# A hybrid decoder block with PEER: other engines for the first conditioning parts and for the gate table

## The chip, the cores and the metric

The kernel runs on one core of a Trainium2 chip. The metric is the device time of one execution, from the first to the last instruction of the core. Three runs of the kernel before took 2813.15, 2819.97 and 2822.08 us, so the median is 2819.97 us.

## The reference

One decoder layer for 1024 tokens of width 1024 in float32. A condition vector c gives six vectors of shifts, scales and gates. The mixing part runs one projection whose columns are shared by a gated convolution and by window attention; the channel part retrieves, for each token, 8 heads x 16 single-neuron experts out of 128 x 128. Cut to what matters:

```python
cond = silu(c);  mod = cond @ w_ada + b_ada;  sh1, sc1, g1, sh2, sc2, g2 = split(mod, 6)
h  = rms_norm(x, norm1_g) * (1 + sc1) + sh1
b_gate, c_gate, hc, q, k, v = split(h @ w_in)
y_conv = b_gate * conv3_causal(c_gate * hc)
y_attn = window_attention(rms_norm(q), rms_norm(k), v, rel_bias, sinks)   # window 128, bias by T5 buckets
x  = x + g1 * (concat(group_norm(y_conv), group_norm(y_attn)) @ w_out)
h2 = rms_norm(x, norm2_g) * (1 + sc2) + sh2
# PEER: 8 heads, product keys 128 x 128, top 16 of 16384 experts per head
q  = h2 @ wq;  scores with keys[0], keys[1];  top 16 of each;  top 16 of the 256 sums -> eidx, softmax -> g
a  = gelu(u[eidx] . h2)
x  = x + g2 * sum_k (g * a)_k v[eidx_k]
```

## The kernel before

The tokens go through the mixing part in three groups (`front`): 384, 384 and 256. Float32 accuracy comes from splitting an operand into a high part rounded to fp32r and a low part, and summing three fp32r products (H.H, L.H, H.L): that is line 301 for the projections, 864 and 921 for the experts. The retrieval ends in one of two ways. For tokens 0 to 639 all 16384 experts are multiplied (`dense`, from about 1010 us on), with a table of gates that is zero where an expert isn't chosen. For tokens 640 to 1023 the chosen rows of u and v are gathered by GpSimd's indirect DMAs beside the dense part.

**The gate table.** For each of five blocks of 128 tokens, `select` (line 625 on) finds the chosen experts as two indices and a gate, and `spread` (line 715) writes the table. Per token the table is a 128 x 128 matrix, and it is an outer product over the 128 chosen slots: `oi` (slot x first index, one-hot times the gate) as weights and `oj` (slot x second index, one-hot) as moving operand. `make(k)` builds these for four tokens, `multiply(k)` does four matmuls into one PSUM tile `gps` (two buffers), `evict(k)` copies it on ScalarE into `stage`, and after eight k the stage goes out to DRAM (`gd`). A block is thus 32 steps k in four stages, and one stage buffer means that the first eviction of the next stage waits until the DMA of the last one is done. The pattern `HOT = "APVV"` gives the four `oi` of each step to ScalarE (two instructions, lines 735 and 736), GpSimd (one) and VectorE (two tokens, one instruction each, line 738); VectorE also makes `oj` for all four in one instruction (line 742). The `oi` have 8 buffers, two steps' worth.

**The start.** `ada_start` (line 184) computes the first two parts of the modulation. Part 1 (scale) is summed on VectorE from eight 128 x 1024 tiles of w_ada (line 193) and then reduced over partitions on TensorE by a matmul with ones (line 200). Part 0 (shift) goes through TensorE alone: 64 fp32 matmuls with one column each (line 195). Meanwhile GpSimd multiplies x by its inverse norm (line 1086). Then `norm1` writes hH and hL, and the projections of the first group begin. The table of attention biases (`bias_table`, line 207) is made beside these projections: eight fp32 matmuls of 384 columns (line 218), each followed by a VectorE addition of the mask and a DMA.

**What sets the order.** Each engine runs its own instructions strictly in the order in which they stand. A scheduler of the framework sets that order when the program is built, except inside `tc.manual_schedule`, where the order is that of the code (in the kernel before that holds for the steady part of `dense`). The steps of `select` and `spread` are a background task: `bg` advances it by `SPREAD = 0.94` steps per estimated us of projection work of the next group, so that the table of group 1's blocks is written beside the projections of group 2 and so on. The order thus fixed does not adapt: where a matmul of `multiply` waits for its `oi`, the projections behind it wait too.

## Time and profile before

| | |
|---|---|
| runs (us) | 2822.08, 2819.97, 2813.15 |
| profiled execution (us) | 2812.93 |
| its span (us) | 2811.2 |
| mean granted TensorE clock | 0.979 |
| PE busy | 2684.1 us, 95% |
| DVE busy | 2287.5 us, 81% |
| ACT busy | 1090.8 us, 39% |
| POOL busy | 1439.0 us, 51% |

PE is TensorE, PEld its weight loads, DVE is VectorE, ACT is ScalarE, POOL is GpSimd. The shares are means over stages with different limits: the dense part is 1.8 of the 2.8 ms. A line of the groups gives engine, operation, out<-in, shapes, the count, then busy us and mean ns of one, then the idle time of the engine just before these instructions and what ended most of it. An fp32 matmul shows as two weight loads and two matmuls.

### The profile page before, as it was taken

Reading aid. Unit: us, or ns where it says so; the run is one execution under the profiler, and the core shown is the slowest. Engines: PE = TensorE matmul, PEld = TensorE weight load, DVE = VectorE, ACT = ScalarE, POOL = GpSimd, SP = SyncE. Lnnn points to the kernel's source line nnn. Section 1 sums busy time; section 2 is a strip of 40 time slices with the busy share of each in tenths; the row PEclk is TensorE's granted clock in tenths of the full one; section 3 lists DMA queues with packets and bytes.
Section 4 is the critical chain, followed back from the end, with each engine's and each line's share of the span. In section 5 each row is a group of like instructions: output and inputs, shape, how many; then the busy total and the mean of one; then the engine's idle time right before and its main releaser. Section 6 shows DMA issues by size and latency. Waiting matters only on the chain.

```text
span 2811.2 us, 45327 instructions
## 1 busy us (share of the span) xinstructions
PE 2684.1 (95%) x15679; PEld 2443.0 (87%) x15679; DVE 2287.5 (81%) x4845; ACT 1090.8 (39%) x2201; POOL 1439.0 (51%) x1323
## 2 busy tenths in 40 slices
PE   8898999999888889999999999999999999999998
PEld 6777989889788788999989899989988899889997
DVE  3664899777987687888988888888888888898886
ACT  2454479774788433232223222322222222222321
POOL 3443433320333145666666566666665666566661
PEclk7999999999999989999999999999999999999999
DMA  7878755677667868999999999999999999999995
GB/s 243 270 245 283 249 198 197 219 256 247 218 212 276 293 224 288 355 329 330 336 341 337 330 360 332 331 332 346 338 314 326 344 340 338 327 337 335 331 332 178
DMA packets 381445, 830.39 MB, mean 295 GB/s; under 512 B 35328, under 2 KB 134048, under 8 KB 378272
## 3 DMA queue, kind: packets, MB, share of 16 engines
q1 hardware_dynamic: 267456, 415.89, 44.6%
q0 software_dynamic: 112320, 408.99, 40.2%
q8 instruction: 123, 2.02, 0.3%
q10 hardware_dynamic: 1440, 2.62, 0.2%
q14 instruction: 106, 0.87, 0.1%
HBM read 746.10 MB, written 81.26 MB: 294 GB/s over the span
## 4 chain that ended last, share of the span: by engine, by line
PE 67%; DVE 13%; DMA 10%; issue 5%; ACT 3%; POOL 2%; SPq 0%; DVEq 0%; ACTq 0%; POOLq 0%
PE pv L921 25%; PE pa L864 23%; PE pj L301 10%; DMA vraw<-in_v 4%; PE gps L750 4%; DMA wraw<-in_wq 2%; DVE pq L816 1%; DVE vdL L908 1%; DVE rows L808 1%; PE pj L310 1%; PE po L477 1%; PE pm L195 1%; DMA rows<-in_u,eidx 1%; DVE gw L883 1%; DMA wt<-in_w_ada 1%
## 5 line engine op out<-in xcount | busy, mean ns | idle before, releaser
L864 PE MATMUL pa<-h,uH 128*128 128x320 f32 x4096 | 776.2, 312 | 16.0 <-ACT uH L847 6.0
L864 PEld LDWEIGHTS pa<-h,uH 128*128 128x128 f32 x4096 | 652.1, 190 | 23.7 <-ACT uH L847 7.0
L921 PE MATMUL pv<-vdH,wdH 128*128 128x512 f32 x1275 | 500.4, 393 | 18.3 <-DVE dacc L940 17.7
L921 PE MATMUL pv<-vdL,wdH 128*128 128x512 f32 x1275 | 498.9, 391 | 0.1
L921 PE MATMUL pv<-vdH,wdL 128*128 128x512 f32 x1275 | 497.9, 390 | 0.0
L864 PE MATMUL pa<-h,uL 128*128 128x320 f32 x2048 | 471.1, 312 | 3.7 <-POOL uL L848 3.7
L848 POOL TENSOR_TENSOR uL<-uraw,uH 128x512 fp32r<-128x512 f32 x256 | 342.3, 1338 | 153.3 <-ACT uH L847 142.7
L789 POOL DMA_INDIRECT rows<-in_u,eidx x257 | 260.7, 1015 | 206.4 <-DVE aw L808 102.7
L738 POOL TENSOR_SCALAR oi<-iota,tr 128x128 f32<-128x128 f32 x160 | 156.0, 976 | 386.1 <-PE gps L750 203.5
L864 PEld LDWEIGHTS pa<-h,uL 128*128 128x128 f32 x2048 | 346.3, 190 | 4.6 <-POOL uL L848 4.6
L789 POOL DMA_INDIRECT rows<-in_v,eidx x254 | 254.9, 1003 | 169.1 <-DVE pq L816 119.4
L940 DVE TENSOR_TENSOR dacc<-dacc,pv 128x512 f32<-128x512 f32 x310 | 212.4, 685 | 147.0 <-PE pv L921 133.5
L816 DVE SCALAR_TENSOR_TENSOR pq<-rows,aw,pq 128x1024 f32<-128x1024 f32 x253 | 324.9, 1284 | 3.8 <-DMA rows<-in_v,eidx 1.1
L907 ACT CAST vdH<-vraw 128x512 fp32r<-128x512 f32 x255 | 153.0, 619 | 445.6 <-DMA vraw<-in_v 393.5
L808 DVE CUSTOM_DVE_ANT_0 rows<-rows,pq 128x1024 f32<-128x1024 f32 x257 | 307.8, 1214 | 11.8 <-issue 8.8
L921 PEld LDWEIGHTS pv<-vdH,wdH 128*128 128x128 f32 x1275 | 240.5, 189 | 73.4 <-DVE dacc L940 24.3
L847 ACT CAST uH<-uraw 128x512 fp32r<-128x512 f32 x256 | 158.2, 619 | 368.0 <-DMA uraw<-in_uT 296.5
L921 PEld LDWEIGHTS pv<-vdH,wdL 128*128 128x128 f32 x1275 | 240.5, 189 | 50.8
L921 PEld LDWEIGHTS pv<-vdL,wdH 128*128 128x128 f32 x1275 | 240.4, 189 | 47.7 <-DVE vdL L908 0.6
L890 ACT CAST wdH<-gw 128x640 fp32r<-128x640 f32 x128 | 93.1, 728 | 424.5 <-DVE gw L883 388.0
L908 DVE TENSOR_TENSOR vdL<-vraw,vdH 128x512 fp32r<-128x512 f32 x255 | 192.8, 773 | 79.7 <-ACT vdH L907 73.0
L280 ACT CAST wH<-wraw 128x512 fp32r<-128x512 f32 x252 | 154.2, 618 | 161.5 <-PE pj L301 74.8
(257 smaller groups left out, 4965.2 us busy)
## 6 DMA issues: line engine op xcount, KB each, us to landing
uraw<-in_uT SPq DMA_DIRECT2D x256, 256.0 KB
vraw<-in_v SPq DMA_DIRECT2D x255, 256.0 KB
gd<-stage SPq DMA_DIRECT2D x20, 2048.0 KB
gt<-gd SPq DMA_DIRECT2D x160, 256.0 KB
wraw<-in_w_in SPq DMA_DIRECT2D x108, 256.0 KB
wraw<-in_wq SPq DMA_DIRECT2D x96, 256.0 KB
wt<-in_w_ada SPq DMA_DIRECT2D x40, 512.0 KB
wL<-low_w_in SPq DMA_DIRECT2D x72, 256.0 KB
```

The costliest lines, as they stand in the source:

```text
L280: A.copy(wH, w)
L301: PE.matmul(pt[:, 0:T], wl[:, c, :], sr[h][:, c, 0:T], start=(h == 0 and c == 0 and k == 0), stop=(h == 1 and c == 3 and k == 2))
L738: (G if who == "P" else V).tensor_scalar(oi, iota, tr[:, 0, t:t + 1], tr[:, 2, t:t + 1], op0=ALU.is_equal, op1=ALU.mult)
L789: G.indirect_dma_start(out=r, out_offset=None, in_=table, in_offset=bass.IndirectOffsetOnAxis(ap=eidx[:, ti, k:k + 1], axis=0))
L808: V.tensor_tensor_reduce(out=r, in0=r, in1=h2, op0=ALU.mult, op1=ALU.add, scale=1.0, scalar=0.0, accum_out=aw[:, k:k + 1])
L816: V.scalar_tensor_tensor(acc, r, aw[:, k:k + 1], acc, op0=ALU.mult, op1=ALU.add)
L847: A.copy(uH, raw)
L848: G.tensor_tensor(uL, raw, uH.bitcast(F32), op=ALU.subtract)
L864: PE.matmul(AT[j][:, s, 0:n], l[:, c, :], h2[r][4 * h + c][:, s * n:s * n + n], start=(h == 0 and c == 0 and k == 0), stop=(h == 1 and c = ...
L908: V.tensor_tensor(vL, raw, vH.bitcast(F32), op=ALU.subtract)
L921: PE.matmul(pt, l[:, P * tt:P * tt + P], r, start=(m == 0), stop=(m == 3 * J - 1))
L940: V.tensor_tensor(dst, dst, pt, op=ALU.add)
```

## The change

**The start.** Both first parts of the modulation are summed on VectorE, part 1 first, then part 0; only the two reductions by ones stay on TensorE. The order is that of the code (`manual_schedule`). The bias table moves into the start: the mask becomes a 33rd row of the contraction, ScalarE copies the eight results into tiles that are idle then, and eight DMAs on SP store them behind the loads of w_ada and the first half tile of w_in. The multiplication of x by its inverse norm on GpSimd is gone; `norm1` of group 0 does it on VectorE, with a share of the low parts on ScalarE and GpSimd. The table `stat` is 136 columns wide in place of 640.

**The gate table.** The gate is split into an fp32r high and a low part (`parts`). Each `oi` becomes a pair, one-hot times high and one-hot times low, in fp32r, and each token takes two fp32r matmuls that add up in PSUM in place of one fp32 matmul. Who makes them: tokens 0 and 1 of a step come from VectorE in two instructions (`hots`, bf16, 256 elements; `two`, 512 elements); token 2 from two GpSimd instructions; token 3 from two GpSimd instructions in even steps and from four ScalarE instructions in odd steps. `oi` now has 3 buffers (pairs), `two` has 2. `top` shares its buffers with `bits`. The dense part stays in code and order.

The diff, cut to its core:

```diff
-    def ada_start(ap, ring, acc):
-
-        mps0 = pm.tile([P, 8], F32, name="pm")
-        for c in range(NC):
-            w1, w0 = ring[2 * c % len(ring)], ring[(2 * c + 1) % len(ring)]
-            nc.sync.dma_start(w1, a["w_ada"][1, :, c, :])
-            nc.sync.dma_start(w0, a["w_ada"][0, :, c, :])
-            if c == 0:
-                V.tensor_scalar(acc, w1, cond[:, c:c + 1], None, op0=ALU.mult)
-            else:
-                V.scalar_tensor_tensor(acc, w1, cond[:, c:c + 1], acc, op0=ALU.mult, op1=ALU.add)
-            for m in range(NC):
-                PE.matmul(mps0[:, m:m + 1], w0[:, P * m:P * (m + 1)], cond[:, c:c + 1],
-                          start=(c == 0 and m == 0), stop=(c == NC - 1), skip_group_check=True)
-            yield
...
-        for h in range(NH):
-            bp = pm.tile([P, 384], F32, name="pm")
-            PE.matmul(bp, rb[:, h, :], bkt, start=True, stop=True)
-            bt = ap.tile([P, 384], F32, name="bt", bufs=1)
-            V.tensor_add(bt, bp, bmask)
-            nc.sync.dma_start(biasd[:, h, :], bt)
-            yield
+        V.memset(rb, 1.0)
+        V.tensor_copy(rb[0:32], relb.unsqueeze(2).to_broadcast([32, NH, P]))
+        bts = [tmp("q") for _ in range(4)] + [tmp("y", bufs=4) for _ in range(4)]
+
+        def fill():
+            for h in range(NH):
+                bp = pm.tile([P, 384], F32, name="pm")
+                PE.matmul(bp, rb[:, h, :], bkt, start=True, stop=True)
+                A.copy(bts[h], bp)
+
+        def store():
+            for h in range(NH):
+                nc.sync.dma_start(biasd[:, h, :], bts[h])
+
+        return fill, store
+
+    def ada_start(ring, accs):
+
+        b0 = COLS["b"][0]
+        mps = [pm.tile([P, 8], F32, name="pm") for _ in range(2)]
+
+        def total(i):
+            for m in range(NC):
+                PE.matmul(mps[i][:, m:m + 1], accs[i][:, P * m:P * (m + 1)], ones[:, 0:1],
+                          start=True, stop=True)
+
+        n = 0
+        for i in (1, 0):
+            for c in range(NC):
+                wt = ring[n % len(ring)]
+                nc.sync.dma_start(wt, a["w_ada"][i, :, c, :])
+                if c == 0:
+                    V.tensor_scalar(accs[i], wt, cond[:, c:c + 1], None, op0=ALU.mult)
+                else:
+                    V.scalar_tensor_tensor(accs[i], wt, cond[:, c:c + 1], accs[i], op0=ALU.mult, op1=ALU.add)
+                if c == NC - 1 and i:
+                    total(1)
+                n += 1
+                yield n
+        total(0)
+        V.tensor_add(mod[:, 8:16], mps[1], cols[:, b0 + 8:b0 + 16])
+        V.scalar_tensor_tensor(gs[:, 0:8], mod[:, 8:16], 1.0, colr("g1"), op0=ALU.add, op1=ALU.mult)
+        yield n + 1
+        V.tensor_add(mod[:, 0:8], mps[0], cols[:, b0:b0 + 8])
+        done.extend((1, 0))
...
-            if scaled:
-                x = chunk(c)
-                A.activation(h, x, AF.Identity, scale=gsc(c), bias=shc(c))
-                V.tensor_scalar(t, x, gsc(c), shc(c), op0=ALU.mult, op1=ALU.add)
-                (G if c % 2 else V).tensor_tensor(lo, t, h.bitcast(F32), op=ALU.subtract)
+            V.scalar_tensor_tensor(t, chunk(c), gsc(c), r[:, 0:T], op0=ALU.mult, op1=ALU.mult)
+            A.activation(h, t, AF.Identity, bias=shc(c))
+            if shared and c % 2:
+                A.activation(t, t, AF.Identity, bias=shc(c))
+                G.tensor_tensor(lo, t, h.bitcast(F32), op=ALU.subtract)
             else:
-                V.scalar_tensor_tensor(t, chunk(c), gsc(c), r[:, 0:T], op0=ALU.mult, op1=ALU.mult)
-                A.activation(h, t, AF.Identity, bias=shc(c))
                 V.scalar_tensor_tensor(lo, t, shc(c), h.bitcast(F32), op0=ALU.add, op1=ALU.subtract)
...
-        tr = gb.tile([P, 3, P], F32, name="tr", bufs=2)
-        A.copy(tr, tps)
-        ng = gb.tile([P, 2, P], F32, name="ng", bufs=1)
-        A.activation(ng, tps[:, 0:3:2, :], AF.Copy, scale=-1.0)
+        tr = gb.tile([P, 2, P], F32, name="tr", bufs=1)
+        A.copy(tr, tps[:, 0:2, :])
+        parts = gb.tile([P, 2, P], F32, name="parts", bufs=1)
+        A.copy(parts[:, 0, :].bitcast(F32R), tps[:, 2, :])
+        V.tensor_tensor(parts[:, 1, :], tps[:, 2, :], parts[:, 0, :], op=ALU.subtract)
+        tri = gb.tile([P, P], BF16, name="tri", bufs=1)
+        A.copy(tri, tps[:, 0, :])
         n, per = P // 4, TB // 4
         made, outs, stages = {}, {}, {}
 
         def make(k):
-            ois = []
-            for x in range(4):
+            t = 4 * k
+            hots = gb.tile([P, P, 2], BF16, name="hots", bufs=1)
+            V.tensor_tensor(hots, iotas, tri[:, t:t + 2].unsqueeze(1).to_broadcast([P, P, 2]), op=ALU.is_equal)
+            two = gb.tile([P, 2, 2, P], F32R, name="two", bufs=2)
+            V.tensor_tensor(two, hots.rearrange("p i x -> p x i").unsqueeze(1).to_broadcast([P, 2, 2, P]),
+                            parts[:, :, t:t + 2].unsqueeze(3).to_broadcast([P, 2, 2, P]), op=ALU.mult)
+            ois = [two[:, :, x, :] for x in range(2)]
+            for x in (2, 3):
                 t = 4 * k + x
-                oi = gb.tile([P, P], F32, name="oi", bufs=8)
-                who = pat[t % len(pat)]
-                if who == "A":
-                    A.activation(oi, iota, AF.Abs, bias=ng[:, 0, t:t + 1])
-                    A.activation(oi, oi, AF.Relu, scale=ng[:, 1, t:t + 1], bias=tr[:, 2, t:t + 1])
+                oi = gb.tile([P, 2, P], F32R, name="oi", bufs=3)
+                if x == 3 and k % 2:
+                    one = gb.tile([P, P], F32, name="one", bufs=1)
+                    A.activation(one, iota, AF.Abs, scale=-1.0, bias=tr[:, 0, t:t + 1])
+                    A.activation(one, one, AF.Relu, scale=-1.0, bias=ones[:, 0:1])
+                    for s in range(2):
+                        A.activation(oi[:, s, :], one, AF.Copy, scale=parts[:, s, t:t + 1])
                 else:
-                    (G if who == "P" else V).tensor_scalar(oi, iota, tr[:, 0, t:t + 1], tr[:, 2, t:t + 1],
-                                                           op0=ALU.is_equal, op1=ALU.mult)
+                    for s in range(2):
+                        G.tensor_scalar(oi[:, s, :], iota, tr[:, 0, t:t + 1], parts[:, s, t:t + 1],
+                                        op0=ALU.is_equal, op1=ALU.mult)
                 ois.append(oi)
-            oj = gb.tile([P, 4, P], F32, name="oj", bufs=2)
+            oj = gb.tile([P, 4, P], F32R, name="oj", bufs=2)
             V.tensor_tensor(oj, iota.unsqueeze(1).to_broadcast([P, 4, P]),
                             tr[:, 1, 4 * k:4 * k + 4].unsqueeze(2).to_broadcast([P, 4, P]), op=ALU.is_equal)
             made[k] = ois, oj
@@ -747,7 +767,8 @@
             ps = outs[k] = gp.tile([P, 4, P], F32, name="gps")
             ois, oj = made.pop(k)
             for x in range(4):
-                PE.matmul(ps[:, x, :], ois[x], oj[:, x, :], start=True, stop=True)
+                for s in range(2):
+                    PE.matmul(ps[:, x, :], ois[x][:, s, :], oj[:, x, :], start=(s == 0), stop=(s == 1))
...
-        first = ada_start(ap, slots[0:3] + wide, slots[3])
-        next(first)
-        for h in range(2):
-            nc.sync.dma_start(x0[h][:, :, 0:T0], a["xT"][:, 4 * h:4 * h + 4, 0:T0])
+        fill, store = bias_table(ap)
+        first = ada_start(slots[0:2] + wide, slots[2:4])
 
         def x0c(c):
             return ch(x0, c)[:, 0:T0]
 
-        for _ in range(3):
-            next(first)
-        r0 = norm_stats(x0c, T0)
-        for c in range(NC):
-            G.tensor_tensor(x0c(c), x0c(c), r0[:, 0:T0], op=ALU.mult)
-        for _ in first:
-            pass
-        hs = norm1(*GROUPS[0], x0c)
-        table.append(add(bias_table(ap), 1.0))
+        with tc.manual_schedule(engines=MANUAL):
+            for n in first:
+                if n == 3:
+                    for h in range(2):
+                        nc.sync.dma_start(x0[h][:, :, 0:T0], a["xT"][:, 4 * h:4 * h + 4, 0:T0])
+                    fill()
+                    pt0 = pj.tile([P, TM], F32, name="pj")
+                    for c in range(NC):
+                        sq = tmp("sq")
+                        A.activation(sq[:, 0:T0], x0c(c), AF.Square)
+                        PE.matmul(pt0[:, 0:T0], onesd, sq[:, 0:T0], start=(c == 0), stop=(c == NC - 1))
+                    r0 = tmp("rstd", bufs=2)
+                    A.activation(r0[:, 0:T0], pt0[:, 0:T0], AF.Sqrt, bias=epsc)
+                if n == 2 * NC + 1:
+                    V.reciprocal(r0[:, 0:T0], r0[:, 0:T0])
+            split()
+            store()
+            hs = norm1(*GROUPS[0], x0c, r0)
         rest.append(add(ada((2, 4, 3, 5), ap, slots), ADA_RATE, ADA0))
...
+    env["iotas"] = env["gb"].tile([P, P, 2], BF16, name="iotas")
+    A.copy(env["iotas"], iota.unsqueeze(2).to_broadcast([P, P, 2]))
```

TensorE at the start, the kernel before (`wt`, `wringa`, `wringb` are w_ada tiles, `cond` the vector, `rb` and `bkt` the bias table, `hH` and `wH` the first projection):

```order
L195 MATMUL pm<-cond,wt 128x1 x8
L310 MATMUL pj<-sq,onesd 128x384 x7
L195 MATMUL pm<-cond,wringa_142 128x1 x8
L310 MATMUL pj<-sq,onesd 128x384
L195 MATMUL pm<-cond,wringb_144 128x1 x8
L195 MATMUL pm<-cond,wt 128x1 x16
L195 MATMUL pm<-cond,wringa_143 128x1 x8
L195 MATMUL pm<-cond,wringb_145 128x1 x8
L200 MATMUL pm<-ones,wt 128x1 x8
L195 MATMUL pm<-cond,wt 128x1 x8
L218 MATMUL pm<-bkt,rb 128x384 x4
L301 MATMUL pj<-hH_285,wH 128x384
```

The one-column matmuls of part 0 stand between everything else, and four bias-table matmuls just ahead of the first projection. The same place after the change:

```order
L196 MATMUL pm<-bkt,rb 128x384 x8
L1111 MATMUL pj<-sq,onesd 128x384 x8
L212 MATMUL pm<-ones,wt 128x1 x16
L312 MATMUL pj<-hH_284,wH 128x384
L312 MATMUL pj<-hL_286,wH 128x384
L312 MATMUL pj<-hH_284,wL 128x384
```

The 64 matmuls of line 195 are gone, all eight of the bias table stand first, and the projection follows the two reductions.

TensorE in the first block of the gate table, before (four tokens of one step, then projections of group 1):

```order
L750 MATMUL gps_3698<-oj_3659,oi_3650 128x128
L750 MATMUL gps_3698<-oj_3659,oi_3653 128x128
L750 MATMUL gps_3698<-oj_3659,oi_3655 128x128
L750 MATMUL gps_3698<-oj_3659,oi_3657 128x128
L301 MATMUL pj_4021<-hL0_2228,wH_3950 128x384
L301 MATMUL pj_4021<-hH0_2226,wL_3951 128x384
L301 MATMUL pj_4021<-hH0_2226,wH_3950 128x384
```

After the change, near the same place (three steps, then projections; x4 and x2 count instructions of one form in a row):

```order
L771 MATMUL gps_3634<-oj_3606,two_3598 128x128 x4
L771 MATMUL gps_3634<-oj_3606,oi_3600 128x128 x2
L771 MATMUL gps_3634<-oj_3606,oi_3603 128x128 x2
L771 MATMUL gps_3676<-oj_3632,two_3621 128x128 x4
L771 MATMUL gps_3676<-oj_3632,oi_3623 128x128 x2
L771 MATMUL gps_3676<-oj_3632,oi_3626 128x128 x2
L771 MATMUL gps_3701<-oj_3674,two_3666 128x128 x4
L771 MATMUL gps_3701<-oj_3674,oi_3668 128x128 x2
L771 MATMUL gps_3701<-oj_3674,oi_3671 128x128 x2
L312 MATMUL pj_4076<-hH0_2176,wL_3993 128x384
L312 MATMUL pj_4076<-hH0_2176,wH_3992 128x384
L312 MATMUL pj_4076<-hL0_2178,wH_3992 128x384
```

Each step has 8 instructions in place of 4, and the last four of a step read `oi` tiles, which come from GpSimd (in even steps both, in odd steps one of them, the other from ScalarE).

GpSimd at the same time, before (`kL`, `qL` and `mc` are low parts that the attention and the output projection of the group need):

```order
L738 TENSOR_SCALAR oi<-iota,tr 128x128 x12
L410 TENSOR_TENSOR kL<-k,kH 128x384
L418 TENSOR_TENSOR qL<-y,qH 128x384 x4
L738 TENSOR_SCALAR oi<-iota,tr 128x128 x46
L402 TENSOR_TENSOR mc_4173<-y,mc_4172 128x384 x4
L738 TENSOR_SCALAR oi<-iota,tr 128x128 x45
```

And after the change:

```order
L758 TENSOR_SCALAR oi<-iota,tr,parts 128x128 x36
L419 TENSOR_TENSOR kL<-k,kH 128x384
L427 TENSOR_TENSOR qL<-y,qH 128x384 x4
L758 TENSOR_SCALAR oi<-iota,tr,parts 128x128 x140
L411 TENSOR_TENSOR mc_4254<-y,mc_4253 128x384 x4
L758 TENSOR_SCALAR oi<-iota,tr,parts 128x128 x118
```

The instructions for `oi` on GpSimd go from 160 to 480 over the whole kernel; `kL` and `qL` of group 1 come behind 36 of them in place of 12.

## Rows read from the trace of the kernel before

**Rows 1.** Table by stage; busy us of each engine (instructions), clock, DMA, GB/s.

```profile
0.00:54.00 54.00, 40.27 (x168) 33.64 (x168) 23.49 (x33) 14.48 (x25) 16.59 (x16) 0.73 0.72 249
...
375.00:645.00 270.00, 257.24 (x1720) 234.18 (x1719) 222.68 (x700) 219.66 (x529) 104.47 (x105) 0.99 0.61 215
...
730.00:920.00 190.00, 170.74 (x1333) 158.25 (x1332) 156.53 (x528) 155.27 (x378) 70.55 (x75) 0.98 0.68 235
...
1010.00:2811.00 1801.00, 1773.28 (x9887) 1612.70 (x9885) 1544.63 (x2091) 479.86 (x783) 1099.29 (x1017) 0.99 0.93 323
```

**Rows 2.** Instructions of line 750 by block; ns min/median/max, first and last start.

```profile
L750 PE MATMUL gps<-oj,oi x256: 271/275/377, 376.6 to 447.4; 128*128 128x128 f32 x128
...
L750 PE MATMUL gps<-oj,oi x256: 270/275/377, 462.2 to 542.2; 128*128 128x128 f32 x128
...
L750 PE MATMUL gps<-oj,oi x256: 270/275/581, 556.4 to 645.0; 128*128 128x128 f32 x128
...
L750 PE MATMUL gps<-oj,oi x256: 270/275/377, 733.5 to 805.2; 128*128 128x128 f32 x128
...
L750 PE MATMUL gps<-oj,oi x256: 270/275/377, 826.7 to 915.6; 128*128 128x128 f32 x128
```

**Rows 3.** Groups of instructions by form, 375 to 920 us.

```profile
L750 PE MATMUL gps<-oj,oi 128*128 128x128 f32 x1280 | 184.1, 281 | 15.6 <-ACT stage L756 12.6 <-DVE oj L742 2.1 <-DVE oi L738 0.3
...
L738 POOL TENSOR_SCALAR oi<-iota,tr 128x128 f32<-128x128 f32 x160 | 156.0, 976 | 386.1 <-PE gps L750 203.5 <-ACT tr L722 169.9 <-DVE mx L453 7.5
L742 DVE TENSOR_TENSOR oj<-iota,tr 128x512 f32<-128x512 f32 x160 | 111.6, 703 | 13.2 <-PE gps L750 12.3 <-ACT tr L722 0.6
L738 DVE TENSOR_SCALAR oi<-iota,tr 128x128 f32<-128x128 f32 x320 | 105.6, 368 | 28.5 <-PE gps L750 27.2
...
L698 DVE TENSOR_TENSOR hot<-hot 128x256 bf16<-128x256 bf16 x10 | 2.9, 288 | 0.2
```

**Rows 4.** Timeline of PE (start us, us) in two stretches of block 0.

```profile
420.98 2.04 PE L750 MATMUL gps<-oj,oi 128*128 128x128 f32 x16
...
430.28 1.90 PE L477 MATMUL po<-vv,pT 128*128 128x64 f32 x16
```

**Rows 5.** Timeline of PEld: weights of fp32r matmuls with 128 columns.

```profile
594.81 0.19 PEld L544 LDWEIGHTS pm<-identr,h2L 128*128 128x128 f32 x1 [0.29 <-DVE h2L L331]
594.92 0.19 PEld L544 LDWEIGHTS pm<-identr,h2H 128*128 128x128 f32 x1
```

**Rows 6.** The critical chain in order of time: start us, us, what.

```profile
301.50 8.32 PE pj L301 x48
...
849.74 8.25 DMA gd<-stage
```

**Rows 7.** Timelines of POOL at three places.

```profile
421.78 3.34 POOL L738 TENSOR_SCALAR oi<-iota,tr 128x128 f32<-128x128 f32 x2 [0.48 <-PE gps L750]
...
494.31 2.13 POOL L738 TENSOR_SCALAR oi<-iota,tr 128x128 f32<-128x128 f32 x2 [3.24 <-PE gps L750]
...
565.67 0.79 POOL L738 TENSOR_SCALAR oi<-iota,tr 128x128 f32<-128x128 f32 x1 [0.46 <-PE gps L750]
```

**Rows 8.** Timelines of DVE at the last two of these places.

```profile
495.00 0.68 DVE L742 TENSOR_TENSOR oj<-iota,tr 128x512 f32<-128x512 f32 x1
...
565.83 0.83 DVE L742 TENSOR_TENSOR oj<-iota,tr 128x512 f32<-128x512 f32 x1 [0.50 <-PE gps L750]
```

**Rows 9.** Timelines of PE and DVE in the start.

```profile
38.35 3.55 PE L200 MATMUL pm<-ones,wt 128*128 128x1 f32 x16
...
48.86 5.48 PE L218 MATMUL pm<-bkt,rb 32*128 32x384 f32 x8 [3.54 <-DVE rb L215]
54.27 0.69 PE L301 MATMUL pj<-hH,wH 128*128 128x384 f32 x1
...
26.52 1.19 DVE L193 SCALAR_TENSOR_TENSOR wt<-wringb,cond,wt 128x1024 f32<-128x1024 f32 x1
```

**Rows 10.** DMA from 0 to 60 us, in 40 slices of 1.5 us.

```profile
GB/s 0 89 221 375 306 352 266 385 412 420 401 410 412 404 421 257 317 410 306 183 210 328 377 372 272 277 68 0 0 0 27 259 63 0 126 237 117 311 264 336
```

More of the change, by code (lines that the diff above doesn't have):

```diff
@@ L50 @@
 TB = 32
-HOT = "APVV"
 RATE0, RATE = 0.0, 0.49
@@ L143, in hymba_peer_kernel @@
     V.memset(upv, 0.0)
-    stat = t1.tile([P, 5, P], F32, name="stat")
+    stat = t1.tile([P, 8 + P], F32, name="stat")
     nc.sync.dma_start(stat, a["stat"])
@@ L224, in hymba_peer_kernel @@
     shifted = bass.AP(tensor=biasd.tensor, offset=biasd.offset + 127,
                       ap=[[NH * 384 - 1, P], [384, NH], [1, 2 * P]])
-    tasks, rest, table = [], [], []
+    tasks, rest = [], []
     def bg(us):
@@ L314, in norm_stats, with norm_mod @@
         return r
-    def norm_mod(chunk, gsc, shc, H, L, T, scaled=False, r=None):
-        if not scaled and r is None:
+    def norm_mod(chunk, gsc, shc, H, L, T, shared=False, r=None):
+        if r is None:
             r = norm_stats(chunk, T)
@@ L348, in group_stats @@
             A.activation(sq, src, AF.Square)
-            PE.matmul(pt[:, 0:T], stat[:, i, :], sq, start=(i == 0), stop=(i == len(chunks) - 1))
+            PE.matmul(pt[:, 0:T], stat[:, 8 - 2 * i:8 - 2 * i + P], sq, start=(i == 0), stop=(i == len(chunks) - 1))
         r = tp.tile([P, TM + 2], F32, name="grs", tag="u", bufs=1)
@@ L639, in select @@
         pairs(8, 8, 1, 56)
-        top = sel.tile([P, PH, 16], F32, name="top")
+        top = sel.tile([P, PH, 16], F32, name="top", tag="bits", bufs=2)
         pu = sel.tile([P, PH, 16], U32, name="pu")
@@ L1158, in _layout @@
         "stat": f(stat),
[L1159 removed]
+        "back": back,
         "iota": f(np.broadcast_to(np.arange(P, dtype=np.float32), (P, P))),
[L1161 to L1162 removed]
+        "bucket": np.concatenate([bucket, np.where(ok, 0.0, NEG)[None]]).astype(np.float32),
     }
```

28 lines of the change are left out of this document (7 added, 21 removed).

## The prediction

> **What bounds the kernel now.** I read the table by stage first. In the dense part TensorE is busy 1773 of 1801 us, and the change leaves that part alone. Of the stages that change, the start has TensorE busy 40.3 of 54 us at a mean clock of 0.73, and the two stretches in which the gate table is written have it busy 257.2 of 270 and 170.7 of 190 us, with VectorE at 222.7 and 156.5, ScalarE at 219.7 and 155.3, and GpSimd at only 104.5 and 70.6 [rows 1]. So TensorE paces the table stretches, two engines are close behind, and GpSimd has room. The second view is the matmuls of line 750, block by block: from the first to the last start the five blocks take 70.8, 80.0, 88.6, 71.7 and 88.9 us, 400 in all for 160 steps, or 2.5 us a step [rows 2]. TensorE's own work for a step is short: 16 weight-and-matmul records span 2.04 us [rows 4], two steps. The rest is projections and attention in between, and a stop every eight steps, where the next eviction waits for the stage's DMA, 8.25 us in the one the chain shows [rows 6]. The third view is GpSimd's `oi`: 160 instructions, mean 976 ns, with 203.5 us of idle time ahead of them that TensorE ended [rows 3]. GpSimd waits for the others there.
>
> **The change part by part.**
>
> *The start.* The first projection begins at 54.27 us, behind the reduction of line 200 (3.55 us), more of line 195 and 5.48 us of bias table [rows 9]. From 12 to 22.5 us the DMA runs at 401 to 421 GB/s and later falls back [rows 10]: the ring of tiles is held up by TensorE's one-column matmuls and by VectorE beside GpSimd's multiplication. After the change VectorE needs 1.19 us for a 512 KB tile when nothing disturbs it [rows 9], and at 410 GB/s a tile takes 1.28 us to load, so the loads should stay ahead at nearly full rate: 16 tiles of 0.52 MB, two of x with 0.79 MB and 0.8 MB of small ones are 10.8 MB, 27 us at 400 GB/s, from about 4 us on. The last tile lands at about 31 us (estimate). Behind it come one VectorE instruction (1.2), the reduction of part 0 (3.55), and three short ones for shift, first chunk and first hH (1.4, estimated): 37 us. The eight stores of the bias table (1.6 MB) and two half tiles of w_in (0.5 MB) stand ahead of, or are, the next weights that the projections need; at 400 GB/s they add 5 us from 31 us on, plus landing and splitting, so I put the real beginning at 40 us: a gain of 14. The four bias-table matmuls that stood between the projections go too; the four ahead of them took 5.48 us in a cold clock, and I count 3 for these. The reciprocal of the norm lies beside the 3.55 us reduction, and the removed GpSimd multiplication was off the path: nothing for either. Start: -17, between -4 (the stores are slow and hold up w_in) and -22.
>
> *The bias load, `stat`, `top`, the copy of `iotas`.* The bias is read later than it is stored in both, the 0.7 MB that no longer load stand in the 10.8, and `top` shares buffers that are free by then. One more ScalarE copy lies beside projections. Nothing; if the cover is gone, 1 us.
>
> *The gate table on TensorE.* One fp32 matmul of 128 columns is two records; now there are two fp32r matmuls, again two records. The pace of a record before is (2.04 - 0.28)/15 = 0.117 us, and matmuls with 64 columns pace at (1.90 - 0.28)/15 = 0.108 [rows 4]. The 0.28 is about one record's own length [rows 3]. Half the columns, nearly the same pace: the weight load sets it. Two consecutive loads of fp32r weights for 128 columns start 0.11 us apart too [rows 5]. So I take 0.11, and the gain over 1280 records is at most 1280 x 0.007 = 9 us; I take 0. If weight loads weren't the limit, 128 fp32r columns would take about 0.066 us (48 matmuls of 384 columns take 8.32 us, 0.173 each [rows 6], and a third of the columns at the same rate plus some overhead), and 1280 x 0.05 = 64 us of TensorE time would go.
>
> *The gate table on GpSimd.* In every two steps there are now six `oi` instructions in place of two, 96 in a block in place of 32. The form is the same (128 x 128, two scalars per partition), so the row's mean holds: 96 x 0.976 = 93.7 us a block [rows 3]. That is more than each block takes today. GpSimd can't work ahead of its need, because three `oi` buffers are one and a half steps: when the stage's DMA stops the evictions, it finishes about eight instructions, 7.8 us, and stands idle for the rest of some 9 us. Four stops a block at 1.5 us make 6. A block then takes 100 us, paced by GpSimd, with TensorE waiting in its fixed order and the projections behind it. Five blocks: 500 against 400, +100 us. GpSimd's mean need not hold. Undisturbed it takes 0.79 us [rows 7]; then a block is 75.8 + 4 x 2.7 = 87, and the sum +33. Where VectorE runs one two-operand instruction after the other, two in a row took 3.34 us, 1.67 each [rows 7]; 1.2 over a block gives 120, and +200. Below nothing it can't go by this, since blocks that GpSimd doesn't pace are paced by TensorE as now, but for the 12.6 us that TensorE spends ahead of line 750 waiting for an eviction [rows 3]. I take the mean, as it is over all 160 of the same form under today's VectorE load.
>
> *The gate table on VectorE and ScalarE.* VectorE per step before: `oj` 0.703 and two `oi` at 0.368, 1.44 us. After: `hots` like the bf16 row of 256 elements, 0.288, `two` and `oj` at 0.703 each, 1.69 [rows 3]. The 0.25 us over 160 steps are 40 us, which count only if VectorE paces; at 3.1 us a step it doesn't. But all three have two operands in SBUF, where two of three had one, so GpSimd will meet them more often. Rows 7 and 8 show such a meeting: an `oj` that began at 495.00 on VectorE, and a pair on GpSimd from 494.31 that took 2.13 us in place of 1.58. This is what the upper bound is for. ScalarE makes four instructions of `oi` in two steps as before. Nothing.
>
> One rule of the Trainium skill speaks against the change harder than my sum. The page "SBUF — State Buffer" (Who interferes with whom) states that a VectorE instruction with two SBUF inputs and a GpSimd instruction that reads SBUF exclude each other, and that the later one fully blocks until the first is finished. The trace agrees in the direction that costs GpSimd time, but not in the length: an `oj` that began 0.16 us into a GpSimd `oi` of 0.79 us took 0.83 in place of 0.68, so it waited 0.15 and not 0.63 [rows 7, 8].
>
> *The sum.* 2812.93 - 17 + 100 = 2896 for the profiled execution, which lies 7 us below the median of the runs; for the median 2903.
>
> **The rivals.** *A, GpSimd fits in.* The evictions' stops leave it enough time and TensorE still paces the blocks; then only the start counts, with perhaps a few us of eviction waits: 2820 - 17 = 2803, faster. For it: the 203.5 us GpSimd idles now. Against it: 320 more instructions of 0.79 us are 253 us, and three buffers can't use idle time that comes in one piece. *B, the fp32r passes halve TensorE's time.* Then 64 us go, but only where TensorE paces; with GpSimd at 100 us a block nothing of it shows. Both together would give 2740. Against it rows 4 and 5. *C, VectorE and GpSimd exclude each other* for the whole of each instruction: a step holds 3 x 0.79 + 1.69 = 4.06 us, a block 130, five 650, +250: 3050. For it the pair at 421.78, against it the `oj` at 565.83. *D, GpSimd paces, but barely*: near its undisturbed 0.79 us, 87 us a block: 2820 - 17 + 33 = 2836, still slower. The point from which the sign turns is 17 us of extra table time, 3.4 us a block; between 80 and 83.4 us a block GpSimd's instruction would have to take 0.74 us at most, less than the undisturbed 0.79. *E, the clock.* TensorE at 75% busy in the start had a mean clock of 0.73 [rows 1]; with waits of about a third in the blocks it could fall between its levels of 1.2 and 2.4 GHz as well, which stretches the projections that run while evictions are stopped. At 2 us for each of 20 stops that adds 40 to the forecast: 2943; it is inside my range.
>
> **How the numbers follow.** The forecast with E has a chance of 0.65 and its own range is 2850 to 2975. D 0.14, A 0.12, B 0.02, C 0.07. A measurement of this kernel tells 0.3%, 8.5 us, from no change. Faster are A and B but for the cases where the start gives less, 0.12; D, with the start at -4, stays above 2828; the same takes 0.04 from the seams of A and D, and slower is 0.84. The range leaves out most of A and B and most of C: 2812 to 2985.
>
> **What would show it.** Line 771 takes 95 to 110 us a block, and GpSimd's idle time ahead of `oi` falls from 386 us to well under 150, while TensorE's before line 771 is ended by GpSimd's line 758, some 100 us in all. GpSimd's `oi` have a mean of 0.9 to 1.1 us. The records of line 771 stay 0.11 us apart. The first projection matmul starts at 36 to 42 us, and VectorE's w_ada instructions take 1.2 to 1.3 us. The dense part keeps its 1801 us within 5. It would be wrong if TensorE waits for ScalarE's `stage` and not for `oi`, or if blocks stay at 80 us: then GpSimd had room that I don't see.

## The result and the profile after

The changed kernel takes 3041.26 us (median of four runs, 3032.48 to 3052.19), the kernel before beside it 2820.04 (four runs). The ratio is 1.0796, with a 95% interval of 1.0762 to 1.0829: slower, as forecast, but by 221 us and not by 83, and above the range.

The profiled execution took 3052.19 us with a span of 3050.4, which is 239.2 more than the span of before. The starts of the table's matmuls divide this: the first comes at 363.1 us in place of 376.6 (-13.5); the five blocks take 638.0 us from first to last start in place of 400.0 (+238.0) [rows 2]; the four stretches between blocks take 149.7 in place of 139.0 (+10.7); what follows the last block takes 1899.6 in place of 1895.6 (+4.0). Nearly all that went wrong lies in the blocks.

The start and the dense part came as forecast. Here are PE's timeline in the start, VectorE's group of w_ada instructions there, and the dense part in the table by stage; they answer to [rows 9] and the last of [rows 1].

```profile
34.69 3.57 PE L212 MATMUL pm<-ones,wt 128*128 128x1 f32 x16 [5.83 <-DVE wt L223]
39.69 0.69 PE L312 MATMUL pj<-hH,wH 128*128 128x384 f32 x1 [1.43 <-ACT hH L335]
```

```profile
L223 DVE SCALAR_TENSOR_TENSOR wt<-wringa,cond,wt 128x1024 f32<-128x1024 f32 x5 | 6.4, 1285 | 5.4 <-DMA wringa<-in_w_ada 5.3
```

```profile
1250.00:3050.00 1800.00, 1770.55 (x9867) 1607.06 (x9865) 1547.19 (x2084) 477.32 (x779) 1099.81 (x1014) 1.00 0.92 322
```

The reduction of part 0 ends at 38.3 us, the first projection begins at 39.69 (forecast 40), and a w_ada instruction takes 1.285 us. In the dense part TensorE is busy 1770.6 of 1800 us at full clock.

Now the blocks. First line 771 in block 0 (ns min/median/max, first and last start), then the table by stage with one row for each block: busy us of PE, PEld, DVE, ACT and POOL, with instruction counts, then the clock, the DMA share and GB/s.

```profile
L771 PE MATMUL gps<-oj,two x128: 222/415/516, 363.1 to 487.6; 128*128 128x128 f32 x128
...
L771 PE MATMUL gps<-oj,oi x128: 272/415/477, 364.8 to 489.7; 128*128 128x128 f32 x128
```

```profile
363.00:490.00 127.00, 105.05 (x447) 92.91 (x446) 90.18 (x296) 61.59 (x154) 101.63 (x99) 0.62 0.24 86
511.00:639.00 128.00, 107.67 (x541) 95.63 (x540) 83.26 (x177) 69.29 (x170) 102.34 (x98) 0.77 0.35 123
652.00:783.00 131.00, 110.51 (x515) 95.89 (x514) 77.67 (x175) 68.98 (x156) 93.17 (x92) 0.75 0.49 168
875.00:1001.00 126.00, 103.96 (x538) 94.09 (x537) 94.12 (x336) 66.91 (x170) 103.22 (x99) 0.65 0.33 113
1022.00:1151.00 129.00, 107.18 (x593) 98.49 (x593) 77.34 (x152) 67.94 (x156) 104.32 (x99) 0.75 0.50 173
```

Block 0 takes 126.6 us from 363.1 to 489.7, where it took 70.8. GpSimd is busy about 101 us of each block, so it is the fullest engine but for TensorE's records, which are longer since the granted clock fell: 0.62 to 0.77, where the stretches of before had 0.98 and 0.99 [rows 1]. The median record of line 771 went to 0.415 us here, from 0.275 [rows 2]. The sums over the five windows, before and after:

```profile
sum 400.00, PE 372.46 PEld 340.38 DVE 335.67 ACT 333.87 POOL 165.12; mean PE 74.49 PEld 68.08 DVE 67.13 ACT 66.77 POOL 33.02
...
sum 641.00, PE 534.36 PEld 477.02 DVE 422.57 ACT 334.71 POOL 504.67; mean PE 106.87 PEld 95.40 DVE 84.51 ACT 66.94 POOL 100.93
```

So the added 241 us can be read from two sides. TensorE has 162 us of longer records, about as many as before, and 79 us more of waiting. GpSimd has 340 us more of work in the same time. Neither engine is busy all the time, so neither reading alone shows which of them sets the pace. The groups of instructions over the whole run:

```profile
L758 POOL TENSOR_SCALAR oi<-iota,tr,parts 128x128 fp32r<-128x128 f32 x480 | 501.2, 1056 | 298.6 <-ACT parts L732 186.1 <-PE gps L771 112.3
...
L771 PE MATMUL gps<-oj,oi 128*128 128x128 f32 x640 | 179.5, 362 | 79.2 <-POOL oi L758 71.9 <-ACT oi L755 6.2
...
L771 PE MATMUL gps<-oj,two 128*128 128x128 f32 x640 | 152.1, 333 | 20.8 <-DVE oj L762 11.1 <-ACT stage L777 6.6 <-DVE two L744 1.5
...
L744 DVE TENSOR_TENSOR two<-hots,parts 128x512 fp32r<-128x512 bf16 x160 | 114.8, 718 | 80.0 <-PE gps L771 77.7
L762 DVE TENSOR_TENSOR oj<-iota,tr 128x512 fp32r<-128x512 f32 x160 | 111.7, 703 | 57.0 <-PE gps L771 54.4 <-ACT tr L730 2.2
L777 ACT COPY stage<-gps 128x512 f32<-128x512 f32 x160 | 90.9, 580 | 89.9 <-PE gps L771 87.9 <-DMA gd<-stage 1.4
```

GpSimd's `oi` has a mean of 1.056 us (976 ns before [rows 3]), 501 us in all. In 112 us it waited for line 771 to free one of its three buffers. The 186 us "until `parts`" lie ahead of the blocks' first steps, where there is no `oi` to make yet, and cost nothing. Two waits of the first kind on POOL's timeline, the longest of all second, and then PE's timeline at the first:

```profile
470.89 1.91 POOL L758 TENSOR_SCALAR oi<-iota,tr,parts 128x128 fp32r<-128x128 f32 x2 [9.03 <-PE gps L771]
...
717.69 5.05 POOL L758 TENSOR_SCALAR oi<-iota,tr,parts 128x128 fp32r<-128x128 f32 x3 [15.69 <-PE gps L771]
```

```profile
458.16 0.41 PE L457 MATMUL pm<-kH,qH 64*128 64x256 f32 x1
...
464.49 0.52 PE L312 MATMUL pj<-hH,wH 128*128 128x384 f32 x1
464.81 0.52 PE L312 MATMUL pj<-hL,wH 128*128 128x384 f32 x1
...
467.37 0.52 PE L312 MATMUL pj<-hH,wH 128*128 128x384 f32 x1
...
469.78 0.56 PE L771 MATMUL gps<-oj,two 128*128 128x128 f32 x4
```

From 458 to 469.8 us TensorE's fixed order holds no matmul of the table, only attention and projections. GpSimd fills its three buffers and stands still for 9.03 us. The projections that it waits for come 0.32 us apart (464.49 to 464.81), where 48 of them took 8.32 us before, 0.173 each [rows 6]: TensorE is at the lower of its two levels, with a granted clock of 0.50 from 458 to 468 us. The wait of 15.69 us shows that the clock isn't needed for such a stop: from 702 to 717.7 us the granted clock is 0.94, and TensorE is busy 15.36 of 15.7 us, most of it with work other than the table's.

### The profile page after: what moved, and what is told of

Its sections match the earlier page's. It is cut to its first block, busy times and chain, and to the rows that moved or that the text cites. A ratio compares the mean times of both kernels' runs of the same rounds, so it can differ in the third digit from the quotient of the medians.

```text
span 3050.4 us, 45576 instructions
## 1 busy us (share of the span) xinstructions
PE 2837.1 (93%) x15567; PEld 2569.0 (84%) x15567; DVE 2376.5 (78%) x4851; ACT 1097.2 (36%) x2219; POOL 1778.1 (58%) x1635
## 4 chain that ended last, share of the span: by engine, by line
PE 60%; POOL 11%; DVE 10%; DMA 10%; issue 6%; ACT 2%; SPq 1%; POOLq 0%; DVEq 0%; ACTq 0%
PE pv L942 21%; PE pa L885 20%; PE pj L312 12%; POOL oi L758 9%; DMA vraw<-in_v 4%; PE gps L771 3%; DVE vdL L929 1%; DVE pq L837 1%; DMA uraw<-in_uT 1%; DVE rows L829 1%; DMA wraw<-in_wq 1%; PE po L485 1%; PE pm L457 1%; PE pj L321 1%; DVE dacc L961 1%
## 5 line engine op out<-in xcount | busy, mean ns | idle before, releaser
L758 POOL TENSOR_SCALAR oi<-iota,tr,parts 128x128 fp32r<-128x128 f32 x480 | 501.2, 1056 | 298.6 <-ACT parts L732 186.1
L771 PE MATMUL gps<-oj,oi 128*128 128x128 f32 x640 | 179.5, 362 | 79.2 <-POOL oi L758 71.9
```

The lines of the kernel that those rows point to most:

```text
L758: G.tensor_scalar(oi[:, s, :], iota, tr[:, 0, t:t + 1], parts[:, s, t:t + 1], op0=ALU.is_equal, op1=ALU.mult)
L771: PE.matmul(ps[:, x, :], ois[x][:, s, :], oj[:, x, :], start=(s == 0), stop=(s == 1))
```

## The experiments

Three theories went into them. **P**: GpSimd's `oi` pace the blocks, with stops behind TensorE's order. **L**, which is rival C of the prediction: VectorE and GpSimd exclude each other. Its 130 us a block match the measured 127.6, so it had to be tested. **K**: TensorE at its lower clock paces. The run of the new start alone was repeated ten times; each of the other versions ran once, beside four runs of the changed kernel that lie 20 us apart. Code is shown shortened. The scheduler sets a new order for each version, so a version can differ from its neighbour by more than the lines shown. Blocks below are from the first to the last start of the table's matmuls, all five together; before has 400.0 and the changed kernel 638.0.

**The two halves apart.** The new start with the old table, and the old start with the new table.

> The new start alone (conditioning parts on VectorE in the fixed order, bias table on TensorE beside them); the gate table is the old one. All theories of the gate table agree: 14 to 17 us under the kernel before, 2803 to 2806 us. If the time is over 2815, the new start itself costs something later in the program that was not seen.

> The new gate table alone, with the old start. Theory P (GpSimd's 480 oi instructions pace the five blocks, with stops between them): 235 us over the kernel before, about 3055. L (a VectorE and a GpSimd instruction exclude each other) and K (TensorE at the lower clock paces the blocks): the same, 3050 to 3060. Under 3040 would say that the two parts work on each other.

The new start alone: 2801.82 us against 2814.84, ratio 0.9958 (0.9936 to 0.9980), the fastest of the versions that compute the whole reference. Its first projection begins at 39.13 us. The new table alone: 3053.28 against 2814.84, +238. The halves add up within the noise (-13 and +238 against +221 for both), so only the table needs explaining.

**VectorE's two-input instructions replaced.**

```diff
-hots = is_equal(iotas, tri); two = hots * parts      # two inputs each
+for s, x: V.tensor_scalar(two[:, s, x, :], iota, tr[:, 0, t], parts[:, s, t], is_equal, mult)
```

> VectorE's two two-input instructions for tokens 0 and 1 (hots and two) become four one-input tensor_scalar instructions; GpSimd's work is unchanged. P: GpSimd's op gets shorter, 1.06 to about 0.85 us, and 60 to 100 us go: about 2960. L: a step is 3 x 0.79 + 0.70 = 3.07 us in place of 4.06, a block 98 us, about 2890. K: 3041, no change.

GpSimd's group, over the run:

```profile
L758 POOL TENSOR_SCALAR oi<-iota,tr,parts 128x128 fp32r<-128x128 f32 x480 | 472.2, 995 | 287.0 <-ACT parts L732 184.9 <-PE gps L771 101.9
```

3005.94 us, blocks of 604.5 in all. L wanted 98 us a block and has 121: it falls. But P was too hopeful as well, by 46 us: with two of VectorE's three two-input instructions gone, the `oi` still took 0.995 us and not 0.85.

**Fewer `oi` for GpSimd.** `if x == 3 and k % 2` becomes `if x == 3`, so ScalarE makes token 3 in every step.

> Token 3 always on ScalarE: GpSimd has 64 oi instructions a block in place of 96, VectorE the same. P: GpSimd has 68 us of work a block and some 25 us of stops, 93 a block in place of 128: about 2870. L: 2 x 0.79 + 1.69 = 3.27 us a step, 105 a block: about 2928. K: 3041 within 15.

GpSimd's group, over the run:

```profile
L758 POOL TENSOR_SCALAR oi<-iota,tr,parts 128x128 fp32r<-128x128 f32 x320 | 368.0, 1160 | 346.9 <-ACT parts L732 175.0 <-PE gps L771 161.9 <-ACT a L672 5.6
```

2958.75 us, blocks of 559.5. GpSimd's work fell from 100 to 74 us a block, but the blocks only to 112: its waits for TensorE rose from 112 to 162 us. P missed by 89 us. Something beside GpSimd holds the blocks above 100. ScalarE, which took over the work, is busy 85 us of a block here and so not full either.

**More buffers.** `oi` with `bufs=6` in place of 3 (and `XB = 2`, two buffers of x in place of four, to make room), with the table of the change and with ScalarE's share of the last run.

> As the changed kernel with six oi buffers in place of three (paid for with two in place of four buffers of x). P (GpSimd's 480 oi instructions pace the blocks, with stops since three buffers let it lead TensorE by a step and a half): the stops fall from 22 to some 8 us a block: about 2970. L (a step is the sum of VectorE's and GpSimd's instructions, 4.06 us): 3041, no change. K (TensorE at its lower clock paces): within 15 of 3041.

GpSimd's group in the first of the two:

```profile
L758 POOL TENSOR_SCALAR oi<-iota,tr,parts 128x128 fp32r<-128x128 f32 x480 | 516.7, 1088 | 234.0 <-ACT parts L732 187.5 <-PE gps L771 45.6 <-ACT halves L470 0.8
```

> Token 3 always on ScalarE, as the run before it that came to 2959, and six oi buffers (and two of x). In that run GpSimd had 74 us of work a block of 112, and its instruction took 1.16 us in place of 1.06. P: the stops behind TensorE go: 95 to 100 us a block, about 2890. L: with two GpSimd instructions 3.27 us a step or more: no change, 2959. K: no change, 2959.

And in the second:

```profile
L758 POOL TENSOR_SCALAR oi<-iota,tr,parts 128x128 fp32r<-128x128 f32 x320 | 378.8, 1195 | 303.1 <-ACT parts L732 183.3 <-PE gps L771 119.3 <-POOL mc L411 0.2
```

With six buffers the waits for TensorE went from 112 to 46 us, as P said (9 us a block), and the time to 3000.35, by 41 and not by 70. With ScalarE's share too it came to 2933.65, blocks of 530.7, and P missed again, by 44 us. So the short buffers are real, L and K as sole causes are out, and some 106 us a block remain, in which GpSimd makes `oi` for only 76.

**TensorE kept busy.** Ten more matmuls of 128 columns in a step, and then six of 256 columns.

```diff
+for s in range(5 * (x // 2)): PE.matmul(ps[:, x, :], identr, identr, ...)                  # first run
+if x % 2 == 0: 3 x PE.matmul(ps[:, x:x + 2, :], identr, identr over two tokens, ...)        # second run
```

> As the changed kernel with ten more matmuls in each step of the gate table (five ahead of tokens 2 and 3 each, identity times identity, into the region that the token's own passes write anew), to keep TensorE busy while it waits for GpSimd. P: the granted clock of the blocks goes from 0.62-0.77 to near 1.0, the stretches of projections between steps shorten and with them GpSimd's stops: 75 to 100 us less, 2950 to 2965. L: 3041 or more. K: 130 us less or more than that, 2850 to 2910. If the clock stays, the time is 3041 or more under each.

> As the changed kernel with six wider matmuls in each step (three of 256 columns ahead of tokens 0 and 2 each, into the region that these tokens' passes write anew), where ten of 128 columns left the clock at 0.72 though TensorE's records filled 95% of the stretch. P (GpSimd's instructions with stops behind a slowed TensorE): if the clock of the blocks comes to 0.9 or more, 50 to 100 us less, about 2960. K (TensorE at its lower clock paces): 130 us less or more, 2850 to 2910. If the clock stays under 0.8: some 100 to 190 us more than 3041 for the added matmuls.

The stretch from the first to the last block, in each:

```profile
361.00:1387.00 1026.00, 968.66 (x5126) 921.08 (x5125) 518.89 (x1641) 410.38 (x990) 486.33 (x497) 0.69 0.35 120
```

```profile
362.00:1173.00 811.00, 724.79 (x4495) 659.05 (x4495) 525.19 (x1648) 413.72 (x992) 501.21 (x498) 0.89 0.44 152
```

And in the first, one stretch of the third block, then TensorE's timeline just behind it (line 771 has the added matmuls here, line 773 the table's):

```profile
729.00:794.00 65.00, 64.92 (x267) 63.93 (x267) 21.14 (x37) 18.22 (x42) 34.02 (x35) 0.50 0.25 88
```

```profile
795.72 0.28 PE L773 MATMUL gps<-oj,two 128*128 128x128 f32 x1
795.83 0.27 PE L771 MATMUL gps<-identr 128*128 128x128 f32 x1
795.94 0.27 PE L773 MATMUL gps<-oj,two 128*128 128x128 f32 x1
```

The first took 3278.56 us: TensorE's records fill 94% of the stretch and the clock is 0.69. From 729 to 794 us TensorE does not wait at all, busy 64.92 of 65 us with these passes and projections, and stays at 0.50 throughout. The second took 3069.10 at 0.89, just short of what P's number asked for, with blocks of 667.3. So the pace stays undecided by these two; what they show is that the clock can stay at its lower level without any wait, and that holding it up with added matmuls costs more than it gives: GpSimd's wait for TensorE rose to 161 us in the second. The timeline gives the pace of an fp32r pass of 128 columns at the upper level (the clock is 1.00 from 794 to 814 us): 0.11 us.

**Without GpSimd.** VectorE's `two` serves all four tokens: `ois = ois + ois` in place of the loop that makes tokens 2 and 3, so ScalarE's `oi` go as well as GpSimd's.

> As the changed kernel without any oi instruction of GpSimd and ScalarE: tokens 2 and 3 of a step are multiplied with the operands of tokens 0 and 1, so half of the table's rows hold other numbers; TensorE, VectorE's three instructions and the evictions stay as they are. P: all that the table lost goes, about 2800 to 2850 (blocks of 70 to 90 us). K: the blocks stay at 115 us or more, 2980 or more. A time between says how the 238 us divide: what is left over 2803 is TensorE's and VectorE's, what goes is GpSimd's.

The sum over the five blocks in the table by stage, and VectorE's two groups:

```profile
sum 505.00, PE 444.51 PEld 406.60 DVE 399.44 ACT 233.17 POOL 21.06; mean PE 88.90 PEld 81.32 DVE 79.89 ACT 46.63 POOL 4.21
```

```profile
L749 DVE TENSOR_TENSOR oj<-iota,tr 128x512 fp32r<-128x512 f32 x160 | 110.6, 691 | 7.7 <-ACT tr L730 5.6 <-PE gps L758 2.0
L744 DVE TENSOR_TENSOR two<-hots,parts 128x512 fp32r<-128x512 bf16 x160 | 110.2, 689 | 61.7 <-PE gps L758 61.0
```

2892.14 us, blocks of 504.5: between P and K, as the last case of the expectation. The `oi` of GpSimd and ScalarE together are worth 134 us of the 238, and 104 us stand without any of them.

**VectorE or the passes?**

```diff
-hots, two: 0.35 + 0.70 us a step
+two = two one-input instructions;  ois = [two[:, x:x + 1, :] over both passes for x in (0, 1, 0, 1)]
```

> As the run without GpSimd's oi (2892, blocks of 101 us), and VectorE's hots and two (0.35 + 0.70 us a step) replaced by two one-input instructions on tokens 0 and 1 (about 0.6 us together). It leaves out the gates' low parts (the high part goes through both passes) and tokens 2 and 3 have the operands of 0 and 1; TensorE's eight passes of a step stay. V (what the blocks keep over 80 us is VectorE's longer step): blocks of 80 to 88 us, 2805 to 2835. R (it is the fp32r passes of 128 columns and the lower clock that they leave): blocks of 95 us or more, 2865 or more.

And the same kernel with fp32 operands and one multiplication of a token:

```diff
-for s in range(2): PE.matmul(ps[:, x, :], ois[x][:, s, :], oj[:, x, :], start=(s == 0), stop=(s == 1))    # F32R
+PE.matmul(ps[:, x, :], ois[x][:, 0, :], oj[:, x, :], start=True, stop=True)                              # F32
```

> As the run before it that came to 2884 (no oi of GpSimd, VectorE's two one-input instructions, two fp32r passes a token, blocks of 100 us at a clock of 0.78 to 0.92), with one fp32 multiplication a token in place of the two fp32r passes; the low parts and the operands of tokens 2 and 3 are left out as there. R (the fp32r passes cost the clock): clock 0.97 or more in the blocks, blocks of 70 to 90 us as before, 2785 to 2810. If the 100 us a block come from elsewhere in the new step (its operands' buffers, its order): 95 us a block or more, 2865 to 2885.

The first two blocks and the sum over all, with two fp32r passes:

```profile
360.00:454.00 94.00, 82.03 (x461) 74.34 (x461) 76.31 (x300) 42.41 (x96) 6.00 (x5) 0.80 0.33 122
472.00:571.00 99.00, 89.23 (x560) 81.19 (x558) 66.40 (x177) 49.27 (x109) 4.39 (x4) 0.91 0.47 164
...
sum 499.00, PE 437.81 PEld 402.08 DVE 351.66 ACT 232.81 POOL 21.27; mean PE 87.56 PEld 80.42 DVE 70.33 ACT 46.56 POOL 4.25
```

and with one fp32 multiplication:

```profile
364.00:433.00 69.00, 66.78 (x465) 60.03 (x464) 65.63 (x225) 40.36 (x92) 4.90 (x5) 1.00 0.48 169
447.00:530.00 83.00, 80.70 (x571) 74.47 (x571) 72.56 (x230) 54.78 (x128) 4.87 (x4) 1.00 0.52 185
...
sum 406.00, PE 381.85 PEld 351.15 DVE 341.54 ACT 237.39 POOL 20.55; mean PE 76.37 PEld 70.23 DVE 68.31 ACT 47.48 POOL 4.11
```

The matmuls of the table in each, over the run:

```profile
L756 PE MATMUL gps<-oj,two 128*128 128x128 f32 x1280 | 227.0, 305 | 49.3 <-DVE oj L747 30.6 <-ACT stage L762 17.5 <-DVE top L620 0.5
...
L755 PE MATMUL gps<-oj,two 128*128 128x128 f32 x1280 | 187.6, 284 | 16.9 <-ACT stage L761 9.7 <-DVE oj L747 5.0 <-DVE two L743 1.8
```

2884.45 us and blocks of 500.1 with the passes; 2792.38 us and blocks of 406.3 without. In the code only the multiplication and the type of its operands differ, and V falls: VectorE's instructions are the same in both. The two fp32r passes go with 94 us, at clocks of 0.80 and 0.91 in place of 1.00 in these two blocks: by the sums, 56 us of longer records and 37 us more of waiting, of which 26 are for VectorE's `oj`. PE's timelines at the head of block 0 show how it begins; fp32r, then fp32:

```profile
363.92 1.08 PE L756 MATMUL gps<-oj,two 128*128 128x128 f32 x8 [1.21 <-DVE oj L747]
365.42 1.49 PE L756 MATMUL gps<-oj,two 128*128 128x128 f32 x7 [0.42 <-DVE oj L747]
367.70 2.16 PE L756 MATMUL gps<-oj,two 128*128 128x128 f32 x9 [0.79 <-DVE oj L747]
369.65 2.87 PE L358 MATMUL pj<-sq,stat 128*128 128x384 f32 x4
```

```profile
364.24 1.18 PE L755 MATMUL gps<-oj,two 128*128 128x128 f32 x8
365.25 0.81 PE L358 MATMUL pj<-sq,stat 128*128 128x384 f32 x2
365.90 2.04 PE L755 MATMUL gps<-oj,two 128*128 128x128 f32 x16
```

With fp32r, eight records are done in 1.08 us and TensorE waits for VectorE's `oj` (1.21, 0.42, 0.79 us); the four matmuls on `stat` behind take 2.87 us. With fp32, sixteen records run without a wait in 2.04 us, as before [rows 4], and two `stat` matmuls take 0.81.

The timelines also show that the order is not the same. With fp32r the scheduler set several steps of the table in a row ahead of `stat`, faster than VectorE can feed them; with fp32 it set one step, two of `stat`, then two steps. So the 94 us are those of the form together with the order that came with it, and no run keeps the one and changes the other.

**GpSimd with fp32.** The changed kernel with that one multiplication.

> As the changed kernel with one fp32 multiplication of a token, as before, in place of the two fp32r passes: GpSimd, VectorE and ScalarE do all they did, the high part of tokens 2 and 3 and the low part of tokens 0 and 1 are left out of the product. If the fp32r passes let the clock fall and the clock lengthens GpSimd's stops: clock 0.95 or more, blocks of 110 to 113 us, 2960 to 2975. If GpSimd and its three buffers alone set the blocks: 127 us still, 3035 to 3045. If the clock falls here too, the stops do it and not the form of the passes.

The first two blocks and the sum over all, then GpSimd's group:

```profile
366.00:485.00 119.00, 93.69 (x507) 82.01 (x505) 75.24 (x217) 60.85 (x154) 103.62 (x98) 0.86 0.29 104
503.00:621.00 118.00, 94.39 (x514) 82.05 (x514) 84.61 (x233) 66.28 (x167) 102.89 (x97) 0.84 0.35 126
...
sum 603.00, PE 465.35 PEld 412.22 DVE 398.86 ACT 323.60 POOL 499.24; mean PE 93.07 PEld 82.44 DVE 79.77 ACT 64.72 POOL 99.85
```

```profile
L758 POOL TENSOR_SCALAR oi<-iota,tr,parts 128x128 f32<-128x128 f32 x480 | 497.1, 1049 | 267.3 <-ACT parts L732 166.7 <-PE gps L770 95.0 <-PE pj L312 5.4
```

3007.55 us, blocks of 604.1, 121 each: between the two cases named, at a clock of 0.84 to 0.86 and not the 0.95 that the first needed. GpSimd waits for line 770 19 us a block. So with fp32 and GpSimd's waits the clock falls too, and the new `oi` of GpSimd and ScalarE cost about 200 us.

The blocks, all five, in one table:

| us | GpSimd and ScalarE make no `oi` | GpSimd makes 96 a block, ScalarE 32 |
|---|---|---|
| one fp32 multiplication | 406.3 | 604.1 |
| two fp32r passes | 500.1 | 638.0 |

(The left column has two one-input VectorE instructions, the right one `hots` and `two`; with fp32r and these, the left has 504.5, a difference of 4 us, too small for single runs to tell. Each cell has its own order of TensorE's stream.) Either part alone costs 94 or about 200 us; together they cost 238. That the two lie partly under each other fits this, and no run shows it by itself.

## Why the prediction was wrong

Right were the sign, the engine named and the start (39.69 us against 40). GpSimd's `oi` at 0.9 to 1.1 us was right (1.056), and so was the dense part. Rival A, that GpSimd fits in, is refuted by the waits of TensorE for line 758; B by the pace of an fp32r pass at the upper clock, 0.11 us where B needed 0.066; D by 127.6 us a block. Two of the prediction's signs failed: GpSimd's idle time ahead of `oi` is 298.6 us and not well under 150, and TensorE's before line 771 that line 758 ended is 71.9 us and not some 100.

**The step that failed** is the sum of a block, "Four stops a block at 1.5 us make 6. A block then takes 100 us", with the term of 0 for TensorE. By its own terms, over five blocks: the instructions made GpSimd busy for 501 us in place of 480 x 0.976 = 468, +33; the stops took 112 us in place of 30, +82; other work and waits of GpSimd, not in the sum at all, are 638 - 501 - 112 = 25. Together +140, and the blocks take 638 us and not 498.

The stops were not only mis-sized but of another kind. The prediction counted the evictions' waits for the stage's DMA, and these all but vanished: ScalarE stood 1.4 us in the whole run until a stage's DMA was done, and TensorE 6.6 us until an eviction. GpSimd stands still wherever TensorE's order holds a stretch of attention or projections longer than three buffers last, as ahead of 470.89 and 717.69 us. The prediction read the 203.5 us of idle ended by TensorE [rows 3] as waiting that the added work would use up. The run with six buffers shows that this was the place: 46 us in place of 112.

One of the readings behind its upper bound was off. It took the pair of 3.34 us at 421.78 as a stretch in which VectorE runs one two-operand instruction after the other. VectorE's timeline there has four one-input instructions among them:

```profile
422.91 1.11 DVE L738 TENSOR_SCALAR oi<-iota,tr 128x128 f32<-128x128 f32 x4
```

The term of 0 for TensorE was taken at full clock, where it holds: records of fp32r and fp32 pace alike, 0.11 and 0.117 us. The clock did not hold. Without the `oi` of GpSimd and ScalarE the passes, with their order, cost 94 us; in the changed kernel they cost 638.0 - 604.1 = 34. The prediction named the mechanism as E, priced it at 40 for a cause in the waits, and left it out of the predicted time. The runs point to a second cause in the passes themselves: with ten added matmuls a step, TensorE stayed 65 us at the lower level without a wait.

Rival C gave 3050 us, nearer than the forecast, and for the wrong reason. `oj` takes 691 ns in the run in which GpSimd makes nothing and 703 ns in the changed kernel, where GpSimd is busy 505 of 641 us; VectorE is not shut out. That the total came out near is luck.

What stays open: how the 34 or 94 us divide between the clock that TensorE loses by waiting for its operands, what the form of the passes does to it, and the order that the scheduler set with each form. The run with ten added matmuls shows that the clock can stay low under the passes without waits, not that they alone bring it down; no run had fp32r passes of 128 columns at full clock through a block.

## What to carry to other kernels

Idle time of a producer that its consumer ends is not free room: look at the longest stretch in which the consumer's order takes nothing, and at how far the buffers let the producer lead, before counting on it. Another form of a multiplication can pace alike at full clock and still go with a lower clock, and then everything beside it gets slower; price it with the other work of the stretch at both levels of the clock. Where a scheduler sets the order, an edit of one instruction moves others too: compare the order of the two builds before calling a run a test of one thing. A number that fits a rival's forecast is no proof of its mechanism, as 130 us a block was not.
